# A two-layer hybrid decoder trunk on one core: background heads advance first in a step, two chunks ahead of the feed-forward part are turned on DVE, the differential output on TensorE, and the end is cut in halves

## The chip, the cores and the metric

The kernel runs on one core of one Trainium2 chip. The metric is the time of one execution on the device in microseconds (us). The kernel before took 2347.46 us as the median of three runs (2346.2 to 2347.61). A difference of about 0.2%, 4.7 us, is what the measurement can tell from no change.

Five engines matter. TensorE (PE in the rows) does every matrix product and some transposes; PEld is its weight load. VectorE (DVE), ScalarE (ACT) and GpSimd (POOL) do the element-wise work, SyncE (SP) issues nearly all transfers. Each engine takes its instructions strictly in the order in which the program wrote them; the engines wait for each other through semaphores.

## The reference

The model has two layers over 256 positions of width 2048, all in float32. In each layer:

```
h = RMSNorm(x);  P = h @ W_in                     # columns shared out among four mixers
A: forgetting attention, 4 heads x 128            # FoX, "f" names
B: latent attention, 4 heads, rotary part         # MLA, "m" names
C: chunked causal gating unit                     # SGU, "u", "v", "s" names
D: differential attention, 4 heads; its output RMS-normalised, "d" names
x += concat(A, B, C, D) @ W_o                     # W_o: 2048 x 2048
x += CrossAttention(RMSNorm(x), RMSNorm(mem))     # 4 heads, 256 memory tokens, W_co: 512 x 2048
x += (silu(n @ W_gate) * (n @ W_up)) @ W_down     # n = RMSNorm(x), hidden width 5632
```

The output is a last RMSNorm of x.

## The kernel before

**Precision.** PE multiplies in a reduced float32 format (fp32r). To keep accuracy, every operand is split in two: a high half, which is the value rounded to fp32r (ACT writes it: `whi`, `fT_hi`), and a low half, the remainder (DVE subtracts: `wlo`, `fT_lo`). A product is then three matmuls, high by high (L303), high by low weight (L304), low by high weight (L305). So each weight that arrives costs ACT a cast and DVE a subtraction, and PE three passes.

**Units.** `drive` (L227) walks all products of both layers as one list of groups. A group (`gate`, `wco`, ...) makes 256 x 512 results; it is cut into units of two blocks of 128 inner rows. A unit of 512 columns is 12 matmuls of 512 columns on PE. Before unit i is multiplied, the weights of unit i+3 are split (`AHEAD` = 3, `convert` L266). Some groups, `wco` and `wo` among them, leave the subtraction of every other unit to POOL (L283).

**Tasks.** Everything else is written as Python generators, called tasks. After each unit `step` (L193) advances each task to its next `yield`, so a `yield` moves the rest of a task behind one more unit of matmuls. There are two lists: urgent ones, advanced in `step` all of them, and background ones (attention heads), of which the first two advance. In the kernel before, the urgent list is advanced first and the background list after it. What a task emits in a step lands on each engine's queue behind what was emitted before, so these two lists and the yields set the order on every engine.

**Draining.** When a unit needs a chunk of its moving operand that a task has not finished, `need` (L104) drains the task: all that is left of it is emitted at once, ahead of the unit's matmuls.

**From x to a normalised operand.** x lies in four chunks of 512 columns (`x0` to `x3`; the tiles are numbered x_113 to x_116 in the order listings). When a group that adds to x has finished chunk c, `into_x` (L945) adds the result on DVE, and a task `norm_chunk` (L342) begins: step 1 squares the chunk on ACT, step 2 does nothing, and then the chunk is turned (transposed), because PE wants the inner dimension on partitions, and split in high and low halves with the gain multiplied in. There are two ways to turn. `turn` (L414) uses PE: four 128 x 128 transposes into PSUM for half a chunk, ahead of each half's split. `turn_blocks` (L422, chosen by `early`) uses DVE: 16 transposes of 32-row strips, four in a step, into SBUF. Before, `wo` and the feed-forward's `down` use DVE for chunks 0 to 2, and `wco` uses PE for all four. The chunks behind `wco` are called `fT`, those behind `wo` `cT`; their first reader behind `wco` is the group `gate`, which takes chunk 0 in its units 0 and 1, chunk 1 in units 2 and 3, and so on. The four `wco` groups are two units each, in the order c0, c1, c0, c1, c2, c2, c3, c3.

**Heads.** A head of attention (`attend` L486, `attend_memory` L1056) emits scores on PE, a masked maximum on DVE, the exponential on ACT, the reciprocal of the sum on DVE (`inv`), the scaling on ACT (L473), transposes on PE (`fpt` for FoX, `cpt` for the memory heads), a copy on ACT (`cpT`), and the product with the values on PE (`fo`, `co`), with yields in between. `out_v` (L1103) is urgent: it drains its two memory heads and emits their `co`. `finish_diff` (L538) normalises the differential heads' output on POOL and turns it on DVE (`ydT`, 16 transposes).

**End.** `final` (L1179): the last group is finished one half of the rows (t) after the other. `finish` adds chunk 3, squares it on ACT with a sum, reduces, takes the root on POOL, scales the four chunks on ACT, DVE and POOL and has SP issue the four output transfers.

Of the kernel before, what the change touches and what calls it, by code (L numbers as in the profile page):

```python
# [11 lines left out]
F32 = mybir.dt.float32  # L12
F32R = mybir.dt.float32r
I32 = mybir.dt.int32
AF = mybir.ActivationFunctionType
ALU = mybir.AluOpType
# [125 lines left out]
class Kernel:  # L142
# [48 lines left out]
            yield  # L191

    def step(self):  # L193
        for t in list(self.urgent):
            t.step()
        self.urgent = [t for t in self.urgent if not t.done]
        for t in list(self.background)[:2]:
            t.step()
        self.background = deque(t for t in self.background if not t.done)


    def high(self, src, hi, scale=None):
# [139 lines left out]
    def norm_chunk(self, st, c, g, name, early):  # L342

        nc, xs, stats, xc = self.nc, st[0], st[1], self.x[c]
        part = xs.parts[c] = self.split_tile(name)
        for t in range(T):
            self.square_sum(xc[:, t, :], stats[:, t, c : c + 1])
        st[4] += 1
        yield
        yield  # L350
        if early:
            raw = self.slot("xT")
            yield from self.turn_blocks(xc[:], raw)
        for b in range(2):
            tv = raw[:, 2 * b : 2 * b + 2, :] if early else self.turn(xc, 2 * b, 2, "xT")
            self.split_turned(tv, part, 2 * b, self.gains[:, g, 4 * c + 2 * b : 4 * c + 2 * b + 2])
            yield
# [75 lines left out]
    def scores(self, pairs, name="s"):  # L433

        ps = self.bank(name)
        first = True
        for q, off, nk in ((1, 0, S), (0, S, P)):
            for n, (x, y) in enumerate(pairs):
                w = S if x.dtype == F32R else nk
                self.nc.tensor.matmul(ps[:, off : off + w], x[:, q * P : (q + 1) * P], y[:, :w], start=first, stop=(q == 0 and n == len(pairs) - 1))  # L440
                first = False
        return ps

# [94 lines left out]
    def finish_diff(self, l, heads, on, ss, y):  # L538
        nc = self.nc
        for t in heads:  # L540
            t.drain()
        lam_init = 0.8 - 0.6 * math.exp(-0.3 * l)
        rd = self.rms(ss[:], 8, P, "drms")
        nc.gpsimd.tensor_scalar(rd[:], rd[:], 1.0 - lam_init, None, ALU.mult)
        for t in range(T):
            ov = on[:, t, :].rearrange("p (h d) -> p h d", h=4)
            nc.gpsimd.tensor_tensor(out=ov, in0=ov, in1=rd[:, 4 * t : 4 * t + 4].unsqueeze(2).to_broadcast([P, 4, P]), op=ALU.mult)
        yield
        yield
        raw = self.slot("ydT")  # L550
        yield from self.turn_blocks(on[:], raw)
        for b in range(2):
            self.split(raw[:, 2 * b : 2 * b + 2, :], y[0][:, 2 * b : 2 * b + 2, :], y[1][:, 2 * b : 2 * b + 2, :], self.gsm[:, l, 5:6])
            yield


# [524 lines left out]
    def cross(self, l, norm, st, memT, mres):  # L1081
# [48 lines left out]
        for hh in range(2):  # L1130
            yield Group("cv", self.blocks("w_cv", l, hh, 8), 256, memT, False, done_v(hh))
        for c in range(NC):
            yield Group("wco", self.blocks("w_co", l, c), 512, y, False, self.into_x(c, st, 2 + 3 * l, "fT"), hold=0 if c else 1)


    def ffn(self, l, norm, st):
# [41 lines left out]

    def final(self, c, stats):  # L1179
        nc = self.nc  # L1180

        def add(ps, t):
            x = self.x[c][:, t, :]
            nc.vector.tensor_tensor(out=x, in0=ps[t][:], in1=x, op=ALU.add)
            self.square_sum(x, stats[:, t, c : c + 1])
            return x, self.gf[c // 2][:, (c % 2) * 512 : (c % 2 + 1) * 512]

        def whole(ps):
            if c == 0:
                self.gf = [self.slot("gf", shape=(P, 1024)) for _ in range(2)]  # L1190
                for i in range(2):
                    nc.gpsimd.dma_start(self.gf[i][:], self.a["g_final"][:, i * 1024 : (i + 1) * 1024].partition_broadcast(P))
            for t in range(T):
                x, g = add(ps, t)
                nc.gpsimd.tensor_tensor(out=x, in0=x, in1=g, op=ALU.mult)

        def finish(ps, t):
            xc, g = add(ps, t)
            ss = self.sm("rfinss", 1)
            nc.vector.tensor_reduce(ss[:], stats[:, t, :], AX.X, ALU.add)  # L1200
            r = self.rms(ss[:], 1, D, "rfin")
            for i in (0, 1, 2, 3):
                x = self.x[i][:, t, :]
                if i == 1 or (i == 0 and t == 0):
                    nc.scalar.mul(x, x, r[:])
                elif i == 2 and t == 0:
                    nc.gpsimd.tensor_scalar(x, x, r[:], None, ALU.mult)
                elif i == 3:
                    nc.vector.scalar_tensor_tensor(out=x, in0=x, scalar=r[:], in1=g, op0=ALU.mult, op1=ALU.mult)
                else:  # L1210
                    nc.vector.tensor_scalar(x, x, r[:], None, ALU.mult)
                nc.sync.dma_start(self.out[t * P : (t + 1) * P, i * 512 : (i + 1) * 512], x)
        return finish if c == NC - 1 else whole


# [132 lines left out]
```

## Time and profile before

| | |
|---|---|
| median of three runs | 2347.46 us |
| the profiled execution, whole | 2347.7 us |
| its span, first to last instruction | 2346.0 us |
| PE busy | 2324.7 us, 99% |
| DVE busy | 1508.6 us, 64% |
| ACT busy | 1132.2 us, 48% |
| POOL busy | 251.3 us, 11% |
| mean granted clock of TensorE | 0.999 of full speed |
| data moved | 444.24 MB, 189 GB/s on average |

The whole execution is 1.7 us longer than the span of its instructions. A row's length is the time one instruction is seen on its engine; successive instructions overlap a little, so the distance between two starts is what a queue really spends. All rows of layer 0 have their like some 1164 us later in layer 1.

### The profile page before, as it was taken

How to read it: one execution, taken by the hardware profiler on the slowest of the kernel's cores; microseconds unless marked ns; L12 is line 12 of the kernel's file. 1: busy time of each engine (PE TensorE's matmuls, PEld its weight loads, DVE VectorE, ACT ScalarE, POOL GpSimd, SP SyncE). 2: the span in 40 equal slices, each digit the busy share in tenths (PEclk: the TensorE clock that was granted, in tenths of full speed). 3: DMA queues.
4: the chain of work that ended last, by engine and by line, in shares of the span. 5: the costliest groups of instructions: out<-in, count | busy, mean ns of one | idle time of the engine just before them, and what ended most of it. 6: DMA issues, size and time to landing. Idle time of an engine off the chain costs nothing.

```text
span 2346.0 us, 28353 instructions
## 1 busy us (share of the span) xinstructions
PE 2324.7 (99%) x10992; PEld 1950.3 (83%) x10992; DVE 1508.6 (64%) x2175; ACT 1132.2 (48%) x1611; POOL 251.3 (11%) x182
## 2 busy tenths in 40 slices
PE   9999999999999999999999999999999999999998
PEld 8888878888888888888898888798888888888886
DVE  6856687655766446767766666866666664476564
ACT  7656555644443334444455555545444443434443
POOL 1222341100000000000012314411000000000000
PEclk9999999999999999999999999999999999999999
DMA  8654555455455555555545454554555555555643
GB/s 293 223 177 154 186 189 188 164 193 200 179 208 195 189 197 181 196 200 184 203 164 193 161 176 159 201 197 162 197 180 197 202 194 196 197 180 192 221 179 126
DMA packets 69719, 444.24 MB, mean 189 GB/s; under 512 B 8000, under 2 KB 10064, under 8 KB 19920
## 3 DMA queue, kind: packets, MB, share of 16 engines
q1 hardware_dynamic: 67328, 435.52, 52.4%
q0 software_dynamic: 2112, 6.85, 0.9%
q8 instruction: 86, 1.41, 0.2%
q14 instruction: 49, 0.40, 0.0%
q10 hardware_dynamic: 144, 0.06, 0.0%
HBM read 440.30 MB, written 2.10 MB: 189 GB/s over the span
## 4 chain that ended last, share of the span: by engine, by line
PE 88%; DVE 4%; ACT 2%; DMA 2%; issue 1%; POOL 1%; SPq 0%; POOLq 0%; ACTq 0%; DVEq 0%
PE gate L305 7%; PE gate L304 7%; PE gate L303 7%; PE up L305 7%; PE up L304 7%; PE up L303 7%; PE down L303 7%; PE down L305 7%; PE down L304 7%; DVE wlo L210 1%; PE wo L305 1%; PE wo L303 1%; PE wo L304 1%; ACT whi L204 1%; DVE xT L428 1%
## 5 line engine op out<-in xcount | busy, mean ns | idle before, releaser
L210 DVE TENSOR_TENSOR wlo<-raw,whi 128x1024 fp32r<-128x1024 f32 (+3 forms) x764 | 933.5, 1235 | 572.4 <-ACT whi L204 566.2
L204 ACT CAST whi<-raw 128x1024 fp32r<-128x1024 f32 (+2 forms) x828 | 842.3, 1037 | 633.8 <-PE up L305 246.6
L303 PE MATMUL gate<-whi,fT_hi 128*128 128x512 f32 x704 | 274.7, 390 | 0.0
L305 PE MATMUL gate<-whi,fT_lo 128*128 128x512 f32 x704 | 274.0, 389 | 0.0
L304 PE MATMUL gate<-wlo,fT_hi 128*128 128x512 f32 x704 | 273.9, 389 | 0.0
L303 PE MATMUL up<-whi,fT_hi 128*128 128x512 f32 x704 | 273.9, 389 | 0.0
L304 PE MATMUL up<-wlo,fT_hi 128*128 128x512 f32 x704 | 273.9, 389 | 0.0
L305 PE MATMUL up<-whi,fT_lo 128*128 128x512 f32 x704 | 273.9, 389 | 0.0
L303 PE MATMUL down<-whi,hid_hi 128*128 128x512 f32 x704 | 273.9, 389 | 0.0
L304 PE MATMUL down<-wlo,hid_hi 128*128 128x512 f32 x704 | 273.9, 389 | 0.0
L305 PE MATMUL down<-whi,hid_lo 128*128 128x512 f32 x704 | 273.9, 389 | 0.0
L210 POOL TENSOR_TENSOR wlo<-raw,whi 128x1024 fp32r<-128x1024 f32 x64 | 165.3, 2587 | 408.4 <-ACT whi L204 408.2
L428 DVE STREAM_TRANSPOSE hidT<-silu 32x256 f32<-32x256 f32 x352 | 153.3, 436 | 5.7
L305 PEld LDWEIGHTS down<-whi,hid_lo 128*128 128x128 f32 x704 | 132.2, 188 | 27.6
L305 PEld LDWEIGHTS gate<-whi,fT_lo 128*128 128x128 f32 x704 | 132.2, 188 | 27.5
L304 PEld LDWEIGHTS up<-wlo,fT_hi 128*128 128x128 f32 x704 | 132.2, 188 | 27.5
L303 PEld LDWEIGHTS up<-whi,fT_hi 128*128 128x128 f32 x704 | 132.2, 188 | 27.5
L305 PEld LDWEIGHTS up<-whi,fT_lo 128*128 128x128 f32 x704 | 132.2, 188 | 27.3
L304 PEld LDWEIGHTS down<-wlo,hid_hi 128*128 128x128 f32 x704 | 132.2, 188 | 27.3
L303 PEld LDWEIGHTS down<-whi,hid_hi 128*128 128x128 f32 x704 | 132.2, 188 | 27.3
L304 PEld LDWEIGHTS gate<-wlo,fT_hi 128*128 128x128 f32 x704 | 132.2, 188 | 27.2
L303 PEld LDWEIGHTS gate<-whi,fT_hi 128*128 128x128 f32 x704 | 132.2, 188 | 27.2
(426 smaller groups left out, 3347.1 us busy)
## 6 DMA issues: line engine op xcount, KB each, us to landing
raw<-in_w_gate SPq DMA_DIRECT2D x88, 1024.0 KB, 4.8
raw<-in_w_up SPq DMA_DIRECT2D x88, 1024.0 KB, 4.7
raw<-in_w_down SPq DMA_DIRECT2D x88, 1024.0 KB, 4.8
raw<-in_w_o SPq DMA_DIRECT2D x32, 1024.0 KB, 4.8
raw<-in_w_dk SPq DMA_DIRECT2D x8, 1024.0 KB, 5.1
raw<-in_w_dv SPq DMA_DIRECT2D x8, 1024.0 KB, 6.5
raw<-in_w_fq SPq DMA_DIRECT2D x8, 1024.0 KB, 4.9
raw<-in_w_fk SPq DMA_DIRECT2D x8, 1024.0 KB, 4.8
```

The costliest lines, as they stand in the source:

```text
L204: self.nc.scalar.copy(hi, src)
L210: (eng or self.nc.vector).tensor_tensor(out=lo, in0=src, in1=hi.bitcast(F32), op=ALU.subtract)
L303: mm(o, xh, wh, start=(i == 0), stop=False)
L304: mm(o, xh, wl, start=False, stop=False)
L305: mm(o, xl, wh, start=False, stop=(i == len(g.ks) - 1))
L428: self.nc.vector.transpose(o[:, :, :, a, :], src[32 * a : 32 * a + 32, :, :, b, :])
```

## The change

1. `step` advances the two background tasks first and the urgent ones after them.
2. `wco` passes `early` for c < 2: chunks 0 and 1 ahead of `gate` are turned by DVE (`turn_blocks`, 16 transposes each) in place of PE.
3. `norm_chunk` with `early` has one more `yield` between the turning and the split. This holds for the chunks behind `wo` and `down` too.
4. `finish_diff` turns its output on PE (`turn`, twice four transposes) in place of DVE.
5. `scores` no longer widens the second product of an fp32r pair from 128 to 256 columns; only the FoX heads have one such pair.
6. `finish` adds and squares the last chunk in two halves of 256 columns, with one more addition of the two sums, and the transfer of output chunk 1 is issued by ACT instead of SP.

```diff
--- before.py
+++ after.py
@@ -191,12 +191,12 @@
             yield
 
     def step(self):
+        for t in list(self.background)[:2]:
+            t.step()
+        self.background = deque(t for t in self.background if not t.done)
         for t in list(self.urgent):
             t.step()
         self.urgent = [t for t in self.urgent if not t.done]
-        for t in list(self.background)[:2]:
-            t.step()
-        self.background = deque(t for t in self.background if not t.done)
 
 
     def high(self, src, hi, scale=None):
@@ -351,6 +351,7 @@
         if early:
             raw = self.slot("xT")
             yield from self.turn_blocks(xc[:], raw)
+            yield
         for b in range(2):
             tv = raw[:, 2 * b : 2 * b + 2, :] if early else self.turn(xc, 2 * b, 2, "xT")
             self.split_turned(tv, part, 2 * b, self.gains[:, g, 4 * c + 2 * b : 4 * c + 2 * b + 2])
@@ -436,8 +437,7 @@
         first = True
         for q, off, nk in ((1, 0, S), (0, S, P)):
             for n, (x, y) in enumerate(pairs):
-                w = S if x.dtype == F32R else nk
-                self.nc.tensor.matmul(ps[:, off : off + w], x[:, q * P : (q + 1) * P], y[:, :w], start=first, stop=(q == 0 and n == len(pairs) - 1))
+                self.nc.tensor.matmul(ps[:, off : off + nk], x[:, q * P : (q + 1) * P], y[:, :nk], start=first, stop=(q == 0 and n == len(pairs) - 1))
                 first = False
         return ps
 
@@ -547,10 +547,8 @@
             nc.gpsimd.tensor_tensor(out=ov, in0=ov, in1=rd[:, 4 * t : 4 * t + 4].unsqueeze(2).to_broadcast([P, 4, P]), op=ALU.mult)
         yield
         yield
-        raw = self.slot("ydT")
-        yield from self.turn_blocks(on[:], raw)
         for b in range(2):
-            self.split(raw[:, 2 * b : 2 * b + 2, :], y[0][:, 2 * b : 2 * b + 2, :], y[1][:, 2 * b : 2 * b + 2, :], self.gsm[:, l, 5:6])
+            self.split(self.turn(on, 2 * b, 2, "ydT"), y[0][:, 2 * b : 2 * b + 2, :], y[1][:, 2 * b : 2 * b + 2, :], self.gsm[:, l, 5:6])
             yield
 
 
@@ -1130,7 +1128,7 @@
         for hh in range(2):
             yield Group("cv", self.blocks("w_cv", l, hh, 8), 256, memT, False, done_v(hh))
         for c in range(NC):
-            yield Group("wco", self.blocks("w_co", l, c), 512, y, False, self.into_x(c, st, 2 + 3 * l, "fT"), hold=0 if c else 1)
+            yield Group("wco", self.blocks("w_co", l, c), 512, y, False, self.into_x(c, st, 2 + 3 * l, "fT", c < 2), hold=0 if c else 1)
 
 
     def ffn(self, l, norm, st):
@@ -1178,11 +1176,14 @@
 
     def final(self, c, stats):
         nc = self.nc
-
-        def add(ps, t):
+        half = self.const.tile([P, T], F32, name="fhalf") if c == NC - 1 else None
+
+        def add(ps, t, n=1):
             x = self.x[c][:, t, :]
-            nc.vector.tensor_tensor(out=x, in0=ps[t][:], in1=x, op=ALU.add)
-            self.square_sum(x, stats[:, t, c : c + 1])
+            for i in range(n):
+                h = slice(i * 512 // n, (i + 1) * 512 // n)
+                nc.vector.tensor_tensor(out=x[:, h], in0=ps[t][:, h], in1=x[:, h], op=ALU.add)
+                self.square_sum(x[:, h], stats[:, t, c : c + 1] if i == 0 else half[:, t : t + 1])
             return x, self.gf[c // 2][:, (c % 2) * 512 : (c % 2 + 1) * 512]
 
         def whole(ps):
@@ -1195,9 +1196,10 @@
                 nc.gpsimd.tensor_tensor(out=x, in0=x, in1=g, op=ALU.mult)
 
         def finish(ps, t):
-            xc, g = add(ps, t)
+            xc, g = add(ps, t, 2)
             ss = self.sm("rfinss", 1)
             nc.vector.tensor_reduce(ss[:], stats[:, t, :], AX.X, ALU.add)
+            nc.vector.tensor_tensor(out=ss[:], in0=ss[:], in1=half[:, t : t + 1], op=ALU.add)
             r = self.rms(ss[:], 1, D, "rfin")
             for i in (0, 1, 2, 3):
                 x = self.x[i][:, t, :]
@@ -1209,7 +1211,7 @@
                     nc.vector.scalar_tensor_tensor(out=x, in0=x, scalar=r[:], in1=g, op0=ALU.mult, op1=ALU.mult)
                 else:
                     nc.vector.tensor_scalar(x, x, r[:], None, ALU.mult)
-                nc.sync.dma_start(self.out[t * P : (t + 1) * P, i * 512 : (i + 1) * 512], x)
+                (nc.scalar if i == 1 else nc.sync).dma_start(self.out[t * P : (t + 1) * P, i * 512 : (i + 1) * 512], x)
         return finish if c == NC - 1 else whole
```

The names in the listings that follow are those of the tiles; L-numbers of the changed kernel are one or two off those of before. The first place is DVE between the last products of `wco` and the first of `gate`, in layer 0. Before:

```order
L950 TENSOR_TENSOR x_115<-wco,x_115 128x512 x2
L212 SCALAR_TENSOR_TENSOR fT_lo<-xT,gains,fT_hi 128x256 x4
L210 TENSOR_TENSOR wlo<-raw,whi 128x1024
L212 SCALAR_TENSOR_TENSOR fT_lo<-xT,gains,fT_hi 128x256 x2
L210 TENSOR_TENSOR wlo<-raw,whi 128x1024
L950 TENSOR_TENSOR x_116<-wco,x_116 128x512 x2
L212 SCALAR_TENSOR_TENSOR fT_lo<-xT,gains,fT_hi 128x256 x2
L210 TENSOR_TENSOR wlo<-raw,whi 128x1024
```

The same place in the changed kernel, from just behind the addition to x_115:

```order
L429 STREAM_TRANSPOSE xT<-x_113 32x2x4x32 x4
L429 STREAM_TRANSPOSE xT<-x_114 32x2x4x32 x4
L210 TENSOR_TENSOR wlo<-raw,whi 128x1024
L429 STREAM_TRANSPOSE xT<-x_113 32x2x4x32 x4
L429 STREAM_TRANSPOSE xT<-x_114 32x2x4x32 x4
L210 TENSOR_TENSOR wlo<-raw,whi 128x1024
L948 TENSOR_TENSOR x_116<-wco,x_116 128x512 x2
L429 STREAM_TRANSPOSE xT<-x_113 32x2x4x32 x4
L429 STREAM_TRANSPOSE xT<-x_114 32x2x4x32 x4
L212 SCALAR_TENSOR_TENSOR fT_lo<-xT,gains,fT_hi 128x256 x2
L210 TENSOR_TENSOR wlo<-raw,whi 128x1024
L212 SCALAR_TENSOR_TENSOR fT_lo<-xT,gains,fT_hi 128x256 x4
```

Four more transposes of x_113 stand ahead of this piece, and four of x_114 behind it. Before, the low halves of chunks 0 and 1 stood between the additions to x_115 and x_116; now those of chunk 0 are the four of the last row, behind 28 transposes and the addition to x_116, and those of chunk 1 come later still. The two low halves just ahead of them are of chunk 2.

The second place is PE at the second pair of memory heads: `cpt` are their transposes, `co` the product that reads the copy of them. Before:

```order
L304 MATMUL cv<-wlo,memTs_hi 128x256
L305 MATMUL cv<-whi,memTs_lo 128x256
L1078 MATMUL cpt<-ident,cp 128x128 x8
L303 MATMUL wco<-whi,yc_hi 128x512
L304 MATMUL wco<-wlo,yc_hi 128x512
L305 MATMUL wco<-whi,yc_lo 128x512
```

And now:

```order
L304 MATMUL wco<-wlo,yc_hi 128x512
L305 MATMUL wco<-whi,yc_lo 128x512
L1076 MATMUL cpt<-ident,cp 128x128 x8
L1114 MATMUL co<-cpT,cv 128x256 x4
L303 MATMUL wco<-whi,yc_hi 128x512
```

Before, a unit of 12 matmuls stood between the transposes and `co`; now `co` follows at once, and the unit stands ahead of both. The first pair of heads, among the `cv` matmuls, has the same shift, and both happen in each layer.

The third place is DVE at the second FoX head, whose `inv` PE waits for by way of ACT. Before:

```order
L210 TENSOR_TENSOR wlo<-raw,whi 128x1024
L776 SCALAR_TENSOR_TENSOR v<-v,mv,lnw 128x512
L777 SCALAR_TENSOR_TENSOR v<-v,lnr,lnw 128x512
L212 SCALAR_TENSOR_TENSOR yd_lo<-ydT,gsm,yd_hi 128x512
L468 RECIPROCAL inv<-sums 128x2
L212 SCALAR_TENSOR_TENSOR yd_lo<-ydT,gsm,yd_hi 128x512
```

And now:

```order
L774 SCALAR_TENSOR_TENSOR v<-v,mv,lnw 128x512
L775 SCALAR_TENSOR_TENSOR v<-v,lnr,lnw 128x512
L210 TENSOR_TENSOR wlo<-raw,whi 128x1024
L468 RECIPROCAL inv<-sums 128x2
L774 SCALAR_TENSOR_TENSOR v<-v,mv,lnw 128x512
L775 SCALAR_TENSOR_TENSOR v<-v,lnr,lnw 128x512
```

`inv` has moved ahead of the second pair of `v` operations, and the split of the differential output has left its neighbourhood.

## Rows read from the trace of the kernel before

**Rows 1.** The page: engines' busy time, and the chain that ended last.

```profile
PE 2324.7 (99%) x10992; PEld 1950.3 (83%) x10992; DVE 1508.6 (64%) x2175; ACT 1132.2 (48%) x1611; POOL 251.3 (11%) x182
...
PE 88%; DVE 4%; ACT 2%; DMA 2%; issue 1%; POOL 1%; SPq 0%; POOLq 0%; ACTq 0%; DVEq 0%
```

**Rows 2.** What PE waited for: total us, times, longest us.

```profile
PE wo L304 <- DVE wlo L210: 3.5, 4, 1.5
PE fpt L479 <- ACT fp L473: 3.0, 2, 1.5
...
PE fo L500 <- ACT fptt L483: 1.1, 2, 0.6
```

**Rows 3.** Timeline of DVE from wco to gate: start us, length us, idle before.

```profile
444.01 1.22 DVE L210 TENSOR_TENSOR wlo<-raw,whi 128x1024 fp32r<-128x1024 f32 x1 [1.95 <-ACT whi L204]
445.16 0.87 DVE L212 SCALAR_TENSOR_TENSOR fT_lo<-xT,gains,fT_hi 128x256 fp32r<-128x256 f32 x2
...
447.08 1.28 DVE L950 TENSOR_TENSOR x<-wco,x 128x512 f32<-128x512 f32 x2
...
451.06 1.23 DVE L210 TENSOR_TENSOR wlo<-raw,whi 128x1024 fp32r<-128x1024 f32 x1 [1.14 <-ACT whi L204]
...
461.29 0.88 DVE L212 SCALAR_TENSOR_TENSOR fT_lo<-xT,gains,fT_hi 128x256 fp32r<-128x256 f32 x2 [0.51 <-ACT fT_hi L206]
```

**Rows 4.** Timeline of PE there: start us, length us.

```profile
453.14 0.39 PE L305 MATMUL wco<-whi,yc_lo 128*128 128x512 f32 x1
453.37 0.60 PE L419 MATMUL xT<-ident,x 128*128 128x128 f32 x4
...
454.27 0.40 PE L305 MATMUL gate<-whi,fT_lo 128*128 128x512 f32 x1
...
456.57 0.60 PE L419 MATMUL xT<-ident,x 128*128 128x128 f32 x4
...
459.78 0.60 PE L419 MATMUL xT<-ident,x 128*128 128x128 f32 x4
...
460.68 0.40 PE L305 MATMUL gate<-whi,fT_lo 128*128 128x512 f32 x1
```

**Rows 5.** Timeline of DVE behind wo, where chunks are turned on DVE.

```profile
314.08 1.23 DVE L210 TENSOR_TENSOR wlo<-raw,whi 128x1024 fp32r<-128x1024 f32 x1
315.23 5.16 DVE L212 SCALAR_TENSOR_TENSOR cT_lo<-xT,gains,cT_hi 128x256 fp32r<-128x256 f32 x2
320.40 3.58 DVE L428 STREAM_TRANSPOSE xT<-x 32x256 f32<-32x256 f32 x8
324.02 1.22 DVE L210 TENSOR_TENSOR wlo<-raw,whi 128x1024 fp32r<-128x1024 f32 x1
```

**Rows 6.** The line L428: duration ns min/median/max, first and last start.

```profile
L428 DVE STREAM_TRANSPOSE xT<-x x144: 425/436/442, 298.0 to 1513.3; 32x256 f32<-32x256 f32 x144
```

**Rows 7.** A stretch of the end: engines' busy us, PEclk (granted clock), DMA share, GB/s.

```profile
2341.00:2342.00 1.00, 0.00 (x0) 0.00 (x0) 0.45 (x1) 0.00 (x0) 0.00 (x0) 0.50 0.74 279
```

**Rows 8.** Timeline of PE: three starts near the beginning, and the last matmul.

```profile
5.80 0.61 PE L304 MATMUL dq<-wlo,hT_hi 128*128 128x512 f32 x1
6.25 0.40 PE L305 MATMUL dq<-whi,hT_lo 128*128 128x512 f32 x1
6.49 0.39 PE L303 MATMUL dq<-whi,hT_hi 128*128 128x512 f32 x1
...
2336.91 0.39 PE L305 MATMUL down<-whi,hid_lo 128*128 128x512 f32 x1
```

**Rows 9.** Timeline at the second pair of memory heads: PE and ACT.

```profile
427.06 1.04 PE L1078 MATMUL cpt<-ident,cp 128*128 128x128 f32 x8
...
427.85 0.47 PE L303 MATMUL wco<-whi,yc_hi 128*128 128x512 f32 x1
...
427.99 1.08 ACT L1079 COPY cpT<-cpt 128x512 f32<-128x512 f32 x2
```

**Rows 10.** The output transfers on SP: duration ns min/median/max.

```profile
L1212 SPq DMA_DIRECT2D out<-x x8: 332/362/456, 2335.2 to 2341.8; - x8
```

## The prediction

> **What bounds the kernel now.** I read the page first: PE is busy 99% of the span and makes up 88% of the chain that ended last [rows 1]. So time goes up or down only with the number of PE's instructions or with its waits. The list of PE's waits comes next: it is short, and the three entries that this change can touch add up to 7.6 us [rows 2]. That caps what smoother queues can give back: even with all three gone and nothing lost the gain would be 0.3%. What the change can cost is not capped, so I went to the timelines of DVE and PE at each place where instructions move, and above all to the one where DVE gets more work ahead of something that PE needs.
>
> **The wait ahead of gate.** Before, PE transposes the second half of its chunks in between and goes from the last `wco` matmul at 453.14 straight to `gate`; the third matmul of `gate`, the first to read a low half of chunk 0, starts at 454.27 [rows 4]. In the changed kernel that low half stands on DVE behind 28 transposes, as the order shows. I work out when it is ready, on the clock of the trace of before. The prices, taken from start to start: a `wlo` 1.15 us (444.01 to 445.16), and since that row is 1.22 long, I take 0.08 off a row's length elsewhere: two additions to x 1.20, two low halves 0.79 [rows 3]. Eight DVE transposes take 3.62 (320.40 to 324.02) [rows 5]; 144 transposes of just this shape all took 0.425 to 0.442 [rows 6], so this price is firm.
>
> DVE stands at the same point as before until the `wlo` of 444.01, whose cast is not moved. From 445.16 its order is: four transposes (446.97), `wlo` (448.12), additions to x_115 (449.32), eight transposes (452.94), `wlo` (454.09), eight transposes (457.71), `wlo` (458.86), additions to x_116 (460.06), eight transposes (463.68), two low halves of chunk 2 (464.47), `wlo` (465.62), and 0.48 later the first low half of chunk 0: 466.1. DVE is late, not idle, all along, and what it needs from PE and ACT is there. So `gate` reaches its third matmul at 466.1 instead of 454.27, 11.8 us late. The eight half-chunk turns saved on PE in the two layers gain nothing: they end in a longer wait.
>
> A second wait follows. Unit 2 of `gate` reads chunk 1, whose low halves stand behind its own last four transposes and behind what chunks 2 and 3 still want from PE. From the third matmul to the end of the unit is 2.30 us (454.27 to 456.57), so unit 0 ends at 468.4. The turn of chunk 2 then starts, and 1.5 us after a turn's start its low half can begin (459.78 to 461.29) [rows 3, 4]: 469.9, two of them to 470.7, two short sums 0.25, `wlo` to 472.1. Unit 1 with its turn lasts 3.21 (456.57 to 459.78), so chunk 3's turn starts at 471.6, its low halves run from 473.1 to 473.9, `wlo` to 475.05, and chunk 1's first low half is done at 475.5. Before, the matmul that reads it started at 460.68 [rows 4]: 14.8 us late.
>
> **The clock.** This holds if TensorE keeps its 2.4 GHz. With four turns fewer ahead of it (0.45 each, below), its last `wco` matmul and the turn of chunk 2 end near 452, and it stands idle until 462.4, when chunk 0's last transposes (461.87) and a cast have run. The trace shows the granted clock at 0.50, the lower level of 1.2 GHz, in 2341 to 2342, with the last matmul started at 2336.91; and at the beginning matmuls of 512 columns followed each other after 0.45 us (5.80 to 6.25) before they went to 0.24 (6.25 to 6.49) [rows 7, 8]. So I expect unit 0 at half speed: 466.1 plus 4.6 is 470.7, the turn 0.35 slower, low halves of chunk 2 at 472.5 to 473.3, sums and `wlo` to 474.7; unit 1, half speed for its first part, ends at 474.4, then 475.9 to 476.7, `wlo` to 477.85, first low half of chunk 1 at 478.3: 17.6 late. I take 17, between 14.8 and 17.6 and nearer to the second, since the clock may come back earlier in unit 1. Two layers, whose rows are alike: **+34.0 us** (29.6 to 35.2 by these two clocks).
>
> The Trainium skill, "TensorE: Matmul & The Clock Gate", section "Part 1: The HAM clock gate", says that the throttled state is the default and that activity lifts it. By that rule the waits cost 2 x 17.6, without it 2 x 14.8; no stretch of PE's idleness inside this kernel before is long enough to show it, the longest being 1.5.
>
> **Heads first.** Three effects on PE:
> - Memory heads. `co` reads the copies on ACT of what `cpt` has just transposed. Before, 12 matmuls hid that. Now nothing does: PE is ready at 427.85, the first copy starts at 427.99, and the two take 1.08 [rows 9], so the wait is 0.7 if it is for the first copy alone, 1.2 if for both, and up to 2.3 if a cast of 1.1 gets in front on ACT. Behind `co` the whole of PE is queued. I take 0.9, near the single copy, since `co`'s first half needs only that. It happens twice in a layer: **+3.6** (2.8 to 9.2).
> - FoX. `fpt` waited 1.5 in each layer because `inv` stood on DVE behind 16 transposes of `ydT` and the `v` operations. Now `inv` is ahead of the second `v` pair and the transposes are gone, and four units lie between scores and `fpt`: **-3.0** (0 to -3.0) [rows 2]. What is late next there is `fo`, drained right behind the last `fpt` as it was: its 1.1 stays.
> - The chunks behind `wo`. The two low halves that took 5.16 instead of 0.87, beside POOL's work, remain ahead of the late `wlo` [rows 5], and the extra yield puts another pair between the same two `wlo`. At most its 0.79 is added to that wait of 1.5 a layer [rows 2]; if the low halves now miss POOL's work, the wait goes. I take +0.6 a layer, near the full pair, since the rest of that queue is the same: **+1.2** (-3.0 to +1.6).
>
> **The differential output on PE.** A matmul takes 0.23 (453.14 to 453.37); from 453.37 to 454.27 stand one turn and two `gate` matmuls, so a turn costs 0.90 less 0.45, or 0.45 [rows 4]. Four more in all: **+1.8**. POOL's result is due some 11 us after the last `do`, and four units of matmuls cover it; a miss would cost a fraction of a us.
>
> **Scores.** Eight matmuls of 128 instead of 256 columns in fp32r. No row has one so narrow. 512 columns take 0.24 [rows 8]; if the time scales, 128 columns save 0.06 against 256, and if a narrow one took as long as 512 columns it would cost 0.12 more. Both ends: -0.5 to +1.0. I take **0**, which lies between and nearer to the scaling that the wider rows show.
>
> **The end.** Adding and squaring in halves lets ACT start on the first half earlier, but pays a second read of the sum and one more small addition: about -0.1. With ACT issuing chunk 1, SP has one transfer less ahead of the last one, an issue of 0.36 [rows 10]: **-0.4** in all (-0.8 to +0.3). The extra yield behind `down` costs nothing: chunk 3's ten units of matmuls hide it.
>
> **The sum.** The profiled execution took 2347.7 (2346.0 of span and 1.7 around it), 0.2 above the median of the runs. 2347.7 + 34.0 + 3.6 - 3.0 + 1.2 + 1.8 + 0 - 0.4 = 2384.9, so **2384.7** against the median, 1.6% slower.
>
> **Rivals.**
> 1. The clock stays at 2.4 GHz, or is back with the first matmuls: 2 x 14.8 in place of 34.0 gives 2380.3. For it: nothing in this trace shows a drop between matmuls. Against it: a wait of ten us, in which PE has nothing else to do. Chance 0.22.
> 2. More is lost: ACT's casts get in front of the memory heads' copies each time and the half clock lasts through unit 1, with the upper bounds 9.2 and 35.2: about 2392. Chance 0.12.
> 3. Not slower: DVE keeps up and `gate` finds its chunk. Place: DVE between 445 and 454. Price: with no wait the eight turns saved on PE count, -3.6, and 2347.7 + 3.6 - 3.0 + 1.2 + 1.8 - 0.4 - 3.6 is 2347.3, or 2344 without the `co` waits. It decides from the point where the 28 transposes cost no more than DVE's slack ahead of 454.27; but the idle stretches there are 1.95 and 1.14 [rows 3], while 28 transposes take 12.7: they would have to take a quarter of what 144 of them took. Chance 0.04, for an order on the chip that I read wrongly.
>
> **How the numbers follow.** My forecast has 0.62, with an own range of 2380 to 2390. Rivals 1 and 2 widen it on both sides; adding the lower ends of the other terms to rival 1 (`co` 2.8, `wo` -3.0, scores -0.5, end -0.8) gives 2374, and the upper ends to rival 2 some 2394 (2397 if `fpt` still waits). I give 2371 to 2396, which leaves out rival 3 and a wait that is a few us shorter than worked out. Slower by over 0.2% (4.7 us, about what a measurement can tell here) is 0.95; within it 0.03; faster 0.02.
>
> **What would show it.** Right: PE's list of waits is led by `gate` waiting for `fT_lo` or `fT_hi`, in each layer an idle stretch of about ten us and one of some two to three; DVE without idle time for 20 us ahead of it, with groups of four and eight transposes; the granted clock below 1 behind it in two places; `co` waiting for `cpT` four times; `fpt` gone from the list. Wrong: no `gate` among the waits, or stretches under five us there, or new waits of like size elsewhere, at `wo` above all.

## The result, and the profile after

| | before | after |
|---|---|---|
| median | 2347.09 us (4 runs) | 2381.60 us (4 runs, 2379.68 to 2383.30) |
| ratio after to before | | 1.0147, 95% interval 1.0130 to 1.0165 |
| span of the profiled execution | 2346.0 us | 2381.6 us |
| mean granted clock of TensorE | 0.999 | 0.990 |

The change makes the kernel 34.5 us slower (1.5%). The prediction said 2384.7, with a range of 2371 to 2396.

The page of the changed kernel, beside [rows 1] (busy us, share of the span, instructions; the granted clock in 40 slices of 59.5 us):

```profile
PE 2334.1 (98%) x10976; PEld 1957.4 (82%) x10976; DVE 1515.2 (64%) x2211; ACT 1133.8 (48%) x1615; POOL 247.9 (10%) x182
...
PEclk9999999899999999999999999998999999999999
```

PE has 16 instructions fewer and is busy 9.4 us longer. That can only be slower matmuls, and the two slices with an 8 in the row of the clock say where: one in each layer.

The list of PE's waits after (total us, times, longest us), beside [rows 2]:

```profile
PE gate L303 <- ACT fT_hi L206: 25.9, 4, 10.7
PE gate L305 <- DVE fT_lo L212: 6.0, 4, 2.5
...
PE fo L500 <- ACT fptt L483: 1.1, 2, 0.6
...
PE xT L420 <- DVE x L948: 1.0, 2, 0.7
PE co L1114 <- ACT cpT L1077: 1.0, 4, 0.2
PE wo L304 <- DVE wlo L210: 0.2, 1, 0.2
```

`gate` now leads with 31.9 us, and was not in the list before. `fpt` (3.0) is gone, `wo` went from 3.5 to 0.2. New beside `gate` are `co` with 1.0 and `xT` with 1.0: turns of the last chunk behind `wo`, which PE makes, wait for DVE's addition (both waits in layer 0).

PE's timeline between `wco` and `gate` after, beside [rows 4] (start us, length us, in brackets the idle time and what ended it):

```profile
449.91 0.60 PE L420 MATMUL xT<-ident,x 128*128 128x128 f32 x4
461.18 0.80 PE L303 MATMUL gate<-whi,fT_hi 128*128 128x512 f32 x1 [10.67 <-ACT fT_hi L206]
...
464.87 0.80 PE L305 MATMUL gate<-whi,fT_lo 128*128 128x512 f32 x1 [2.47 <-DVE fT_lo L212]
465.47 0.63 PE L303 MATMUL gate<-whi,fT_hi 128*128 128x512 f32 x1
465.89 0.63 PE L304 MATMUL gate<-wlo,fT_hi 128*128 128x512 f32 x1
...
469.31 1.05 PE L420 MATMUL xT<-ident,x 128*128 128x128 f32 x4
...
476.14 0.50 PE L303 MATMUL gate<-whi,fT_hi 128*128 128x512 f32 x1 [2.27 <-ACT fT_hi L206]
...
477.39 0.52 PE L305 MATMUL gate<-whi,fT_lo 128*128 128x512 f32 x1 [0.52 <-DVE fT_lo L212]
```

Two things are to be seen. PE is idle for 10.67, 2.47, 2.27 and 0.52 us; layer 1 repeats it within 0.01 us. And behind the first wait matmuls of 512 columns start 0.42 apart (465.47 to 465.89), where before it took 0.23.

DVE's timeline of the same stretch, beside [rows 3]:

```profile
443.60 1.77 DVE L429 STREAM_TRANSPOSE xT<-x 32x256 f32<-32x256 f32 x4
...
447.86 3.57 DVE L429 STREAM_TRANSPOSE xT<-x 32x256 f32<-32x256 f32 x8
...
452.72 3.58 DVE L429 STREAM_TRANSPOSE xT<-x 32x256 f32<-32x256 f32 x8
...
458.79 3.61 DVE L429 STREAM_TRANSPOSE xT<-x 32x256 f32<-32x256 f32 x8
462.42 0.88 DVE L212 SCALAR_TENSOR_TENSOR fT_lo<-xT,gains,fT_hi 128x256 fp32r<-128x256 f32 x2
463.21 1.21 DVE L210 TENSOR_TENSOR wlo<-raw,whi 128x1024 fp32r<-128x1024 f32 x1
464.34 1.66 DVE L212 SCALAR_TENSOR_TENSOR fT_lo<-xT,gains,fT_hi 128x256 fp32r<-128x256 f32 x4
466.04 1.80 DVE L429 STREAM_TRANSPOSE xT<-x 32x256 f32<-32x256 f32 x4
```

From 443.60 to 467.84 no row of DVE, of those left out either, has an idle stretch ahead of it. The low half that `gate` waits for is the group at 464.34, behind 28 transposes. The high half comes no sooner: ACT, which has to square chunk 3 first, waits 6.83 us for DVE's addition of 457.48, which stands in the same queue, and makes the high halves at 460.62:

```profile
458.25 0.63 ACT L336 ACTIVATE junk<-x 128x512 f32<-128x512 f32 x1 [6.83 <-DVE x L948]
```

The same place in stretches (length, busy us of PE, PEld, DVE, ACT and POOL, granted clock, DMA share, GB/s):

```profile
454.00:461.00 7.00, 0.00 (x0) 0.00 (x0) 6.80 (x14) 2.71 (x6) 0.00 (x0) 0.50 0.32 132
462.00:470.00 8.00, 5.53 (x15) 4.06 (x15) 5.75 (x12) 0.32 (x1) 0.00 (x0) 0.50 0.37 131
471.00:477.00 6.00, 3.61 (x17) 2.46 (x15) 4.40 (x9) 4.26 (x9) 1.60 (x1) 1.00 0.00 0
478.00:481.00 3.00, 3.00 (x8) 2.33 (x8) 0.53 (x2) 0.00 (x0) 0.00 (x0) 0.50 0.88 333
```

The granted clock, 1.00 (2.4 GHz) up to 453, falls to 0.50 (1.2 GHz) while PE is idle, and is back by 471. It falls a second time, around 478 to 481, behind the waits of 2.27 and 0.52 us. By the trace's records the two stretches at 0.50 last 17.1 and 3.4 us, in both layers.

### The profile page after: what moved, and what is told of

Same layout as the page of the kernel before. It is cut to its first block, busy times and chain, and to the rows that moved or that the text cites. A ratio compares the mean times of both kernels' runs of the same rounds, so it can differ in the third digit from the quotient of the medians.

```text
span 2381.6 us, 28333 instructions
## 1 busy us (share of the span) xinstructions
PE 2334.1 (98%) x10976; PEld 1957.4 (82%) x10976; DVE 1515.2 (64%) x2211; ACT 1133.8 (48%) x1615; POOL 247.9 (10%) x182
## 4 chain that ended last, share of the span: by engine, by line
PE 89%; DVE 4%; ACT 2%; issue 2%; DMA 1%; POOL 1%; SPq 0%; POOLq 0%; DVEq 0%; ACTq 0%
PE gate L305 7%; PE gate L303 7%; PE gate L304 7%; PE up L305 7%; PE up L304 7%; PE up L303 7%; PE down L303 7%; PE down L304 7%; PE down L305 7%; PE wo L305 2%; PE wo L303 2%; PE wo L304 2%; DVE xT L429 2%; DVE wlo L210 1%; ACT whi L204 1%
```

## The experiments

Two theories stood at the start. **A**: nearly all of the loss is DVE's queue ahead of `gate`, longer by the two chunks' transposes, with the fallen clock as a second part. **B**: it comes from the changed order as a whole (heads first, the extra yield), and the two chunks are only where it shows. (The expectations of experiments 1 and 2 call B theory C; the other letters in an expectation are its own.)

### 1. The change without the two chunks on DVE

```diff
-... self.into_x(c, st, 2 + 3 * l, "fT", c < 2) ...
+... self.into_x(c, st, 2 + 3 * l, "fT") ...
```

> The changed kernel, but wco's four chunks are all turned on TensorE as before. Theory A (the two DVE-turned chunks are the whole loss, the other parts gain a little): the waits of gate vanish and what is left is what the trace after shows elsewhere, about -4.2 us against before: 2343 us. Theory B (my own terms for the other parts, +3.2 us, hold and hide behind the gate): about 2350 us. Theory C (the reordered heads cause a good part of the loss): above 2355 us.

Measured: 2342.90 us, ratio to before 0.9981 [0.9973, 0.9990]. Its longest waits:

```profile
PE dq L304 <- DVE wlo L210: 1.3, 3, 0.8
PE cq L304 <- POOL wlo L210: 1.2, 2, 0.6
```

`gate` is gone from the list. One argument makes a difference of 38.7 us (2381.6 to 2342.9). All the rest of the change is worth 4.3 us to the good (2.3 to 6.3 by the interval), which theory B can't give, and which the prediction had not either (+3.2).

### 2. The two chunks on DVE alone, in the kernel before

```diff
-... self.into_x(c, st, 2 + 3 * l, "fT") ...
+... self.into_x(c, st, 2 + 3 * l, "fT", c < 2) ...
```

> The kernel before with only chunks 0 and 1 ahead of gate turned on DVE (no extra yield, old order of heads). Theory A1 (DVE's queue alone): the same first wait of about 10.7 and 2.5 us a layer; without the extra yield chunk 1's first low halves stand ahead of chunk 3's, so the second wait of 2.3 us and the second fall of the clock shrink or vanish, some 4 us a layer less: about 2378 us. Theory A2 (the extra yield does not matter here): 2347 + 2 x 19.9 = 2387 us. Theory C (the heads' order is needed for the loss): below 2365 us.

Measured: 2375.64 us, 1.0126 [1.0112, 1.0140]. Its waits begin with

```profile
PE gate L303 <- ACT fT_hi L206: 21.3, 2, 10.7
PE gate L305 <- DVE fT_lo L212: 5.0, 2, 2.5
```

So the first wait is the same to a tenth without any other part: theory A holds for it. But there is no second wait, and the chunks alone cost 28.4 us, not 38.7. Ten us of the loss need another part of the change.

### 3. One chunk instead of two

```diff
-... "fT", c < 2) ...
+... "fT", c < 1) ...
```

> The changed kernel with only chunk 0 turned on DVE ahead of gate, chunk 1 on TensorE. Theory A (DVE's queue): 16 transposes instead of 28 stand ahead of chunk 0's first low half, along with four low halves of chunk 1; by the rows of before it is ready at 462.2 instead of 466.1 on that clock, 7.9 us late, with no second wait, and half speed for a while behind it: 10 to 12 us a layer, 2364 to 2367 us. Rival (it is not the number of transposes but that the chunk is drained at all): as after, about 2380 us.

Measured: 2362.77 us, 1.0069 [1.0055, 1.0082]. PE waits 7.7 and 0.7 us a layer. With 12 transposes fewer on DVE ahead of chunk 0's low half the first wait is 3.0 shorter and the second 1.8, together 4.8; twelve transposes at 0.45 are 5.4. The wait goes with the length of the queue. The time is 1.2 us under the 2364 to 2367 expected.

### 4. and 10. PE kept busy during the waits

Extra matmuls of 128 columns, whose results nobody reads, stand on PE's queue ahead of `gate`'s unit 0 (44) and unit 2 (8). The second of the two kernels has 12 more inside unit 0, between its second and third matmul. Everything else is still computed.

```diff
+            if u.group.name == "gate" and self.fill:
+                self.fill -= 1
+                n = (44, 0, 8)[2 - self.fill % 3]
+                if n:
+                    d = self.bank("fill")
+                    for k in range(n):
+                        self.nc.tensor.matmul(d[:, :P], self.ones[:], self.ones[:], start=(k == 0), stop=(k == n - 1))
...
+                if g.name == "gate" and i == 0 and t == 0 and self.fill == 2:   # the second kernel alone
+                    d = self.bank("fill")
+                    for r in range(12):
+                        self.nc.tensor.matmul(d[:, :P], self.ones[:], self.ones[:], start=(r == 0), stop=(r == 11))
```

> The changed kernel with 44 extra matmuls of 128 columns, whose result nobody reads, ahead of gate's first unit, and 8 ahead of its third, in each layer: they fill most of TensorE's idle time there (about 9.4 and 1.7 us at full clock). Theory D (the clock's fall costs): the granted clock stays at 1.00, units 0 and 1 run at full speed, and the wait of chunk 1 ends earlier: 2.8 to 5 us a layer less, 2372 to 2376 us. Rival (DVE's queue decides everything, the clock is hidden behind it): 2381 us, the same as after.

> The changed kernel with extra matmuls that nobody reads ahead of gate's first unit (44) and third unit (8), and 12 more inside the first unit, where it waits for the low half. Theory D (each us at half speed costs about half a us): the granted clock stays at 1.00 throughout and the 3.4 us a layer at half speed that were left with 56 fewer of them cost 1.7 a layer: 3.4 us less than the 2376.7 of that run, 2373 us. Rival (DVE's queue is what is left, the clock is hidden): 2376 to 2377 us.

Measured: 2376.65 us, 1.0128 [1.0113, 1.0144], and 2372.47 us, 1.0107 [1.0092, 1.0122]. In the first a wait of 2.97 us was left inside unit 0, and behind it the clock stood at 0.50 for 3.4 us, so that the time stayed just above the 2372 to 2376 expected:

```profile
PE gate L315 <- DVE fT_lo L212: 7.0, 4, 3.0
```

In the second the time is what was expected (2373) and the granted clock is 1.00 through this whole place; stretches as above:

```profile
454.00:461.00 7.00, 6.15 (x53) 5.87 (x53) 6.84 (x14) 4.04 (x9) 0.00 (x0) 1.00 0.04 15
462.00:470.00 8.00, 7.71 (x46) 6.65 (x46) 6.00 (x15) 3.20 (x6) 1.60 (x1) 1.00 0.37 131
...
478.00:481.00 3.00, 3.00 (x15) 2.50 (x14) 2.41 (x3) 1.38 (x2) 0.00 (x0) 1.00 0.22 49
```

DVE is as full as before, PE does more work, and the kernel is 9.1 us faster than the changed one: that is the price of the clock, about a quarter of the 38.7. The rows at the lower level agree. In unit 0 ten matmuls take 4.44 (464.87 to 469.31) instead of 2.30, the turn and two matmuls behind it 0.8 more than at the upper level, and eight matmuls from 477.73 on 1.5 more: 4.4 a layer, 8.8 in two. The other 30 us remain with the clock at 1.00: they are DVE's queue.

The Trainium skill, "TensorE: Matmul & The Clock Gate", section "Terms", prices a throttled time at that time multiplied by one less the clock's share. By that rule, as an estimate, the two stretches, 20.5 us a layer, would cost 20.5 us in the two layers; here they cost 9.1, because for more than half of the longer one PE had nothing to do (9.8 of 17.1 us). The measurement decides: here only the matmuls that were due in the stretch counted, and the 8.8 of the rows comes near the 9.1.

### 9. No extra yield for the chunks behind `wco`

```diff
-            yield
+            if name != "fT":
+                yield
```

> The changed kernel without the extra yield in the chunks ahead of gate (kept behind wo and down). Theory A (that yield puts chunk 1's low halves behind chunk 3's and so makes the second wait and the second fall of the clock): both vanish, and the chunks on DVE cost what they cost in the kernel before with part 2 alone, 28.4 us on top of 2342.9: 2371 us. Rival (the second wait comes from the other parts): 2381 us.

Measured: 2371.83 us, 1.0105 [1.0091, 1.0118]. Its list of waits begins with the same two lines as that of experiment 2, number for number, and has no others at `gate`. ACT makes the first high halves of chunk 1 here in the changed kernel (first line) and in this one (second line):

```profile
475.57 1.71 ACT L206 ACTIVATE fT_hi<-xT,gains 128x256 fp32r<-128x256 f32 x4
473.60 0.91 ACT L206 ACTIVATE fT_hi<-xT,gains 128x256 fp32r<-128x256 f32 x2
```

The second wait and the second fall of the clock come from the yield behind the last transposes of chunk 1: with it chunk 1's high halves are made in a step of their own, at 475.57 on ACT, when PE has gone through unit 1 and waits; without it the first pair is made at 473.60. Counted from the turn of chunk 2 on PE (469.31 with, 471.02 without the yield) that is 6.3 and 2.6 us. So part 3 costs 9.8 us at `gate`. Nothing of it showed in experiment 2, where this yield isn't there. (The 9.8 and the 9.1 of experiment 10 can't be added: the second fall of the clock is in both.)

### 5. Heads first, alone

```diff
+        for t in list(self.background)[:2]:
+            t.step()
+        self.background = deque(t for t in self.background if not t.done)
         for t in list(self.urgent):
             t.step()
         self.urgent = [t for t in self.urgent if not t.done]
-        for t in list(self.background)[:2]:
-            t.step()
-        self.background = deque(t for t in self.background if not t.done)
```

> The kernel before with only the order of the two lists in a step turned round. Theory A (it frees inv from the queue behind the urgent tasks): fpt's 3.0 us of waiting go, co waits 4 x 0.24 = 1.0 us: -2.0 us, 2345 us. Rival (fpt waits because of the 16 transposes of ydT on DVE, not because of the order): fpt still waits, only co's 1.0 us comes on top: 2348 us.

Measured: 2348.69 us, 1.0007 [0.9998, 1.0016], no difference that can be told. In its list of waits `fpt` is gone, but `fo` has 2.4 in its place:

```profile
PE fo L500 <- DVE u L789: 2.4, 2, 1.2
...
PE co L1116 <- ACT cpT L1079: 1.0, 4, 0.2
```

Of the 3.0 removed at `fpt`, 1.3 returned one product further on, and 1.0 went to `co`. So the order alone does free `fpt`, as theory A had it, but by these waits only 0.7 us of gain would be left, and the time shows none: it is nearer to the rival's 2348.

### 6. The differential output on PE, alone

```diff
-        raw = self.slot("ydT")
-        yield from self.turn_blocks(on[:], raw)
         for b in range(2):
-            self.split(raw[:, 2 * b : 2 * b + 2, :], ...)
+            self.split(self.turn(on, 2 * b, 2, "ydT"), ...)
```

> The kernel before with only the differential output turned on TensorE. Theory A (order, see the other run): fpt's wait becomes shorter by the 1.8 us of the four transposes that stood in its way and so vanishes as well, 4 turns cost 1.8 us: -1.2 us, 2346 us. Rival (the turns only cost): 2349 us.

Measured: 2350.48 us, 1.0014 [1.0005, 1.0023]: some 3 us slower, with runs from 2347.92 to 2354.20; the trace is of a run of 2348.12, 1.0 us above before, so where the rest of the 3 us goes is not shown. There `fpt` is gone too, and `fo` waits 1.5 twice; `wo` has 4.9 instead of 3.5:

```profile
PE wo L304 <- DVE wlo L210: 4.9, 4, 1.5
PE fo L500 <- ACT fptt L483: 3.0, 2, 1.5
```

### 7. The extra yield, alone

```diff
             yield from self.turn_blocks(xc[:], raw)
+            yield
```

> The kernel before with only the extra yield between turning and splitting. Theory A (the yield is what rids wo of its wait for the late wlo in the changed kernel, because the low halves no longer meet POOL's two subtractions in a row): wo's 3.5 us go to 0.2 to 1, 1.0 us comes on top where the transposes of chunk 3 wait for its addition: about -2 us, 2345 us. Rival (my prediction's term: the wait grows by 0.6 a layer): 2348.4 us. If the wait goes in neither this run nor the one with heads first, it takes both.

Measured: 2341.31 us, 0.9976 [0.9966, 0.9986]. This one line is better than the kernel before by 5.8 us, where theory A expected about 2. Its median is the lowest of all versions here, though the intervals of experiments 1, 11 and 12 overlap its own. Its list of waits has no `wo` in it. DVE, ACT and POOL behind `wo` in this kernel, beside [rows 5]:

```profile
306.68 2.94 ACT L204 CAST whi<-raw 128x1024 fp32r<-128x1024 f32 x3
...
308.74 2.49 POOL L210 TENSOR_TENSOR wlo<-raw,whi 128x1024 fp32r<-128x1024 f32 x1 [5.11 <-ACT whi L204]
309.00 3.60 DVE L429 STREAM_TRANSPOSE xT<-x 32x256 f32<-32x256 f32 x8
312.76 3.36 POOL L210 TENSOR_TENSOR wlo<-raw,whi 128x1024 fp32r<-128x1024 f32 x1 [1.53 <-ACT whi L204]
313.78 3.02 DVE L212 SCALAR_TENSOR_TENSOR cT_lo<-xT,gains,cT_hi 128x256 fp32r<-128x256 f32 x2
...
321.58 1.23 DVE L210 TENSOR_TENSOR wlo<-raw,whi 128x1024 fp32r<-128x1024 f32 x1
```

And ACT and POOL there in the kernel before:

```profile
306.78 1.99 ACT L204 CAST whi<-raw 128x1024 fp32r<-128x1024 f32 x2
310.94 0.91 ACT L206 ACTIVATE cT_hi<-xT,gains 128x256 fp32r<-128x256 f32 x2 [2.17 <-DVE xT L428]
...
313.50 3.08 ACT L204 CAST whi<-raw 128x1024 fp32r<-128x1024 f32 x3
...
314.61 5.49 POOL L210 TENSOR_TENSOR wlo<-raw,whi 128x1024 fp32r<-128x1024 f32 x2 [3.28 <-ACT whi L204]
```

Before, a high half stood on ACT ahead of the casts and waited 2.17 us for DVE's transposes. So the casts came three in a row, POOL got two subtractions in a row, and DVE's two low halves lay beside them: 5.16 us [rows 5]. With the yield ACT casts three times before it meets that wait, POOL's work is spread, and the low halves take 3.02. The other pair, which stood further ahead with 0.89 and a wait of 0.58 for ACT, now follows with 1.12 and no wait: together 4.1 us in place of 6.6. So the late `wlo` starts at 321.58 instead of 324.02, in time for PE. The four waits of 3.5 us in all are gone, and `cq` starts 2.41 us earlier. Some more small steps bring it to 3.5 by `ck` and to 5.8 in the two layers; what they are isn't settled. The trace shows this order of events; no run changes ACT's order without DVE's, so their shares are read from the rows and not from a run of their own.

The Trainium skill, "SBUF — State Buffer", section "SBUF: two separate sides", says that a GpSimd operation that reads SBUF and a DVE operation with two inputs in SBUF lock each other out for a whole instruction. The trace agrees: two low halves beside POOL take 3.02 or 5.16 us, alone 0.88, while eight transposes, which have one input, take 3.60 beside POOL's 2.49.

### 8. The end, alone

```diff
-            xc, g = add(ps, t)
+            xc, g = add(ps, t, 2)
...
-                nc.sync.dma_start(...)
+                (nc.scalar if i == 1 else nc.sync).dma_start(...)
```

> The kernel before with only the end changed (halves, output chunk 1 over ACT). Theory A (the trace after has 8.7 us from the last matmul to the end, as before): no difference, 2347.2 us. Rival (my prediction's term): -0.4 us, 8.3 us from the last matmul to the end.

Measured: 2347.05 us, 0.9999 [0.9990, 1.0008]. No difference. The chain behind the last matmul (2372.50) in the changed kernel:

```profile
2373.38 0.42 ACT L336 ACTIVATE junk<-x 128x256 f32<-128x256 f32 x1 [1.97 <-DVE x L1185]
...
2374.47 0.16 DVE L1202 TENSOR_TENSOR rfinss<-rfinss,fhalf 128x1 f32<-128x1 f32 x1 [0.39 <-ACT junk L336]
...
2375.50 0.88 DVE L1213 TENSOR_SCALAR x<-x,rfin 128x512 f32<-128x512 f32 x2 [0.69 <-POOL rfin L325]
```

The square starts 0.33 sooner behind the last matmul than before, but two halves of 0.42, a second read and the extra addition use it up: scaling starts 3.00 us behind the last matmul, before as after (2336.91 to 2339.91). ACT's issue brings nothing either: from the last matmul's start to the span's end it is 9.1 us in both.

### 11. and 12. The yield with heads first, and with the turn on PE

These are the edits of experiments 7 and 5, and of 7 and 6, together.

> The kernel before with the extra yield and the heads first, nothing else. Theory A (the yield frees wo, and the heads' order trades fpt's 3.0 us for 1.0 at co and 1.3 more at fo): 2341.3 - 0.7 = 2340.6 us. Rival (the effects of the single runs add up, +1.6): 2342.9 us.

> The kernel before with the extra yield and the differential output turned on TensorE, nothing else. Theory A (four turns cost 1.8 us, fpt's 3.0 us go, fo waits 1.9 more): 2341.3 + 0.7 = 2342 us. Rival (the effects of the single runs add up, +3.4): 2344.7 us.

Measured: 2342.59 us, 0.9981 [0.9973, 0.9990], and 2343.81 us, 0.9985 [0.9977, 0.9994]. Neither adds a gain to the yield. The medians lie nearer to the rivals (the single effects add up) than to theory A, but with intervals of some 2 us either way they hardly tell the two apart. At `fpt` and `fo` together PE waits 4.1 us with the yield alone, 2.4 with heads first, 3.0 with the turn on PE, and 1.1 with both (experiment 1, which has parts 5 and 6 as well). So only together do the two edits take the whole 3.0 away; what they save there goes into `co` (1.0) and the four turns (1.8).

Part 5, the narrower scores, was not run by itself. In the rows its three matmuls take 0.440 us after, 0.445 before, start to start.

## Why the prediction was right, and where its sizes were off

The direction, the place and the mechanism were right: `gate` waits for chunk 0 behind DVE's 28 transposes. The time came out 3.1 us below the forecast because two errors of size nearly cancelled, and that is luck: the term at `gate` was 4.7 us too low, all the rest 7.5 too high. Three of the terms fell outside the bounds given for them: `gate`, the chunks behind `wo` and the memory heads.

| term | forecast | measured | by |
|---|---|---|---|
| waits and clock at `gate` | +34.0 (29.6 to 35.2) | +38.7 | after less experiment 1 |
| all the rest | +3.2 | -4.3 | experiment 1 |
| of it the chunks behind `wo` | +1.2 (-3.0 to +1.6) | -5.8 | experiment 7 |
| memory heads | +3.6 (2.8 to 9.2) | +1.0 | list of waits |
| FoX | -3.0 | -3.0 | list of waits, with parts 1 and 4 together |
| differential output | +1.8 | +2.1 (some 3 either way) | experiment 12 less 7, by the ratios |
| scores | 0 | -0.01 a head at most | rows, no run |
| end | -0.4 | -0.1 (-2.3 to +1.9) | experiment 8 |

The single terms below "all the rest" add up to some -5.8, and experiment 1 has -4.3. The difference lies within the intervals; its list also has 1.0 at `xT`, which no term of mine held, and 0.8 at `wo`, and experiment 7 has neither.

- **DVE's queue.** It came as worked out. At this point everything stands 1.55 us earlier than before, by what the rest of the change gains up to there. With that added, the first low half matmul starts at 466.4 on the clock of before, against 466.1 forecast, and chunk 1's at 478.9 against 478.3. The price of 3.62 for eight DVE transposes held: 3.57 to 3.61 here.
- **The clock.** The forecast had it at half speed through unit 0 and a first part of unit 1; it was back at 471, one us into unit 1. The step that was mis-sized is "the clock may come back earlier in unit 1", for which I took 17 where 17.6 stood: the first low half of chunk 1 was 18.3 late. What it lacked altogether is the second fall. I stopped the account at chunk 1's first low half, as though PE ran at full speed from there; eight matmuls at 0.43 put 1.5 more on each layer. That is 19.8 in place of 17; `up` starts 19.9 late.
- **The second wait.** It was forecast, but I put it down to chunk 1's transposes and the turns of chunks 2 and 3. Experiment 9 shows the yield as its condition: without it there is none.
- **Behind `wo`.** Here the step that takes "+0.6 a layer", "since the rest of that queue is the same", failed. Low halves do remain ahead of the late `wlo`, and another pair does come between, but I counted DVE's queue as if ACT's and POOL's instructions stood still. The other case that I named, low halves that "miss POOL's work", came true in part. The yield moved casts on ACT ahead of a wait, and with them POOL's work, and the low halves that took 5.16 us became shorter by 2.1. The gain of 5.8 is more than the 3.5 that stood in the list of waits at `wo`.
- **Memory heads.** The wait is 0.24 us each time, below my lower bound of 0.7. In [rows 9] the first copy starts 0.93 behind `cpt`, since ACT is on other copies from 427.26 to 428.10; after, ACT is free:

```profile
427.71 1.03 PE L1076 MATMUL cpt<-ident,cp 128*128 128x128 f32 x8
...
428.34 1.07 ACT L1077 COPY cpT<-cpt 128x512 f32<-128x512 f32 x2 [1.41 <-PE cpt L1076]
...
428.98 1.99 PE L1114 MATMUL co<-cpT,cv 128*128 128x256 f32 x8 [0.24 <-ACT cpT L1077]
```

  The first copy starts when half of `cpt` is done, 0.63 behind its start, and `co` needs only that copy. My bound took over the delay of an ACT that was busy then.
- **FoX.** The gain of 3.0 came. "What is late next there is `fo`" was right in the whole change and wrong for its parts: either alone moves 1.3 or 1.9 us of the wait to `fo`.
- **The rivals.** The first (the clock stays, 2380.3) fell: the clock did drop, and experiment 10 shows that without it the time would be 2372.5. The second (ACT's casts ahead of the copies each time) fell with the 0.24 at `co`. The third, DVE keeping up, fell with the 10.67.

## What to carry to other kernels

Before moving work onto an engine that is 64% busy on average, list what stands on its queue between the moment its data come and the moment the bounding engine needs the result: here DVE had three us of slack and got 12.7 us of transposes. A wait of PE of that size costs more than its length, since the matmuls behind it ran at half the clock here: 9.1 us on top of 30. And a yield may be worth more than all the moved work (5.8 us here), if it lets an in-order engine pass others' casts before its own wait, but the same line can hurt at another place that runs through it: try it by itself, and at each place by itself.

## What the runs showed of the hardware that was not expected

- The granted clock fell a second time (to 0.50, for 3.4 us) behind waits of only 2.27 and 0.52 us, with 2.9 us of matmuls and a turn at 1.00 ahead of them (470.97 to 473.88). In experiment 4 a wait of 2.97 had the same sequel. None came in experiment 10, with no wait at `gate` over 0.85, and no second one in experiments 2, 3 and 9, where PE has no wait at `gate` once the clock is back.
- At the lower level matmuls of 512 columns start 0.43 us apart, at the upper one 0.23.
- An fp32r product of 128 columns in place of 256 saved 0.005 us over a sequence of three matmuls, 0.440 for 0.445: next to nothing.
- Two low halves on DVE take 0.87 us alone, 3.02 beside one POOL subtraction and 5.16 beside two; eight transposes on DVE took 3.60 beside POOL's 2.49, no more than the 3.57 to 3.61 without.
